# A hybrid encoder trunk: the n2 transform of its long convolution regrouped into pairs on 64x64 quarters of TensorE, in a bound order

## The chip, the cores and the metric

The kernel runs on one core of a Trainium2 chip. The metric is the device time of one execution in microseconds (us), the median of three runs. All numbers are float32; matrix products that must be accurate are done either as plain fp32 matmuls or as three fp32r products of split operands (a high part, and the low part that is left).

## What is computed

Two requests, prompt and sample, go through the same layer with the same weights:

```python
def encoder_layer(x, mem, ...):
    h = rmsnorm(x, norm_g)
    p = h @ w_in
    hy_u, hy_z, cf_a, cf_z, xa_q, xa_z = jnp.split(p, SPLITS, axis=-1)
    k2 = hyena_two_sided_filter(L, ...)
    y_hy = hyena_branch(hy_u, ..., k2, hy_skip) * jax.nn.silu(hy_z)
    y_cf = conformer_branch(cf_a, ...) * jax.nn.silu(cf_z)
    y_xa = memory_attention(xa_q, rmsnorm(mem, mem_norm_g), xa_w_kv) * jax.nn.silu(xa_z)
    mix = jnp.concatenate([y_hy, y_cf, y_xa], axis=-1)
    return x + mix @ w_out

def bidir_fftconv(u, k2, skip):
    uf = jnp.fft.rfft(uf32, n=2 * L, axis=1)
    kf = jnp.fft.rfft(k2, n=2 * L, axis=0)
    y = jnp.fft.irfft(uf * kf[None], n=2 * L, axis=1)[:, :L]
```

L is 2048, the width 1024, the Hyena branch has 512 channels; a last RMSNorm follows. The convolution is over a circle of 2L = 4096 = 64 x 64 positions. The position is 64 n1 + n2, the frequency 64 k2 + k1 (names as in the kernel), so the 4096-point transform is a 64-point transform over n1 with twiddles, and then one over n2. The two requests ride as the real and the imaginary part of one complex signal.

## The kernel before, in words

The program has three stages, one after the other, and a scheduler sets each engine's order within them.

**Stage 1** (lines 204 to 707) multiplies the normed input by `w_in`, 512 tokens at a time: three fp32r matmuls for each of eight pieces of the contraction (`proj`, lines 439 to 441). Work for VectorE (DVE), ScalarE (ACT) and GpSimd (POOL) runs beside it from two queues of closures: the 31-tap convolution, the filter (`filter_background`: a small network, `taps` at line 330, and the filter's transform over n1 at line 355, whose results ACT copies out at line 357 into the DRAM array XF), and at the end eight of the 32 steps of the signal's transform over n1 (`a_background`, line 613).

**Stage 2** (lines 717 to 918) holds three things. Attention (`attention`, line 756) runs in 16 blocks of two half-blocks; each half-block ends with the products of line 792. Between them stand the 24 other steps of the transform over n1 (`stage_a`, line 812): transpose, split, three pairs of products (`times_t1`, line 185), and two copies out of PSUM, one on DVE and one on ACT (line 827), stored to the DRAM array X1. Then comes the transform over n2 (`stage_b`, line 890), 33 steps t. A step loads the filter's column and takes its transform (`spectrum`, line 845: one fp32 matmul of 128x128 by 512 columns, and four half-tile copies on DVE and ACT into kr and ki). Then for column t, and for its mirror 64 - t, `unit` (line 831) does the forward matmul (line 833), two half-tile copies on ACT that swap real and imaginary part (835, 836), two products with kr and ki (838 on DVE, 839 on DVE or POOL), their sum on POOL (840), the inverse matmul (842) and a copy on ACT (843). ACT issues the store to the DRAM array AA (895, 899). SyncE (SP) issues the loads (869). Every third step also loads and splits a piece of `w_out` (`wo_load`, line 855).

The order of one unit is thus a chain over four engines:

```python
            nc.tensor.matmul(u, stab[:, t2, :], x, start=True, stop=True)
            nc.scalar.copy(us[0:64, :], u[64:128, :])
            nc.scalar.copy(us[64:128, :], u[0:64, :])
            nc.vector.tensor_tensor(z, u, kr, op=ALU.mult)
            e2.tensor_tensor(us, us, ki, op=ALU.mult)
            nc.gpsimd.tensor_tensor(z, z, us, op=op)
            nc.tensor.matmul(o, stab[:, t3, :], z, start=True, stop=True)
            nc.scalar.copy(out, o)
```

**Stage 3** (lines 922 to 980) has 32 steps, each for two columns n2 of both requests: the inverse transform over n1 (line 949), transposes (954), the gate, the split of the branch outputs (192 to 194), 48 fp32r matmuls with `w_out` (972 to 974), the residual, the last norm and the store. Its first loads read AA, and so wait for the last store of stage 2.

Of the kernel before, what the change touches and what calls it, by code (L numbers as in the profile page):

```python
# [35 lines left out]
def _tables():  # L36
# [11 lines left out]

    n1 = np.arange(64)
    n2 = np.arange(64)  # L50
# [26 lines left out]
    psi = 2 * np.pi * ((n2[:, None] * n2[None, :]) % 64) / 64  # L77
    cp, sp = np.cos(psi), np.sin(psi)

    def s2(cc, ss):  # L80
        return np.block([[cc, -ss], [ss, cc]])

    def s3(cc, ss):
        return np.block([[cc, ss], [-ss, cc]])

    cpr, spr = cp[:, ::-1], sp[:, ::-1]
    kz = s2(cp, sp)
    kz[64:] = 0
    th = 2 * np.pi * n2[:, None] / 128
    kh = np.zeros((128, 128))  # L90
    kh[64:, :64] = np.cos(th) * cp - np.sin(th) * sp
    kh[64:, 64:] = -np.cos(th) * sp - np.sin(th) * cp

    fr = (4 * np.arange(16)[:, None, None] + np.arange(2)[None, :, None] + 2 * np.arange(2)).reshape(-1)
    fr = np.concatenate([fr, 64 + fr])
    sf = s2(cp, sp)[fr]
    kz, kh = kz[fr], kh[fr]
    stab = np.stack([s2(cp, sp), s2(cpr, spr), s3(cp.T, sp.T), s3(cpr.T, spr.T), kz, kh, sf], axis=1)
# [3 lines left out]
        "stab": stab, "ident": np.eye(128),  # L102
# [5 lines left out]
def kernel(ctx: ExitStack, tc: tile.TileContext, a: dict):  # L108
# [23 lines left out]
    AA = dram.tile([64, 129, 512], F32, name="aa")  # L132
# [39 lines left out]
    def chans(d, g, n):  # L172

        return d[g, :, :, n * 64:(n + 2) * 64].rearrange("k c m -> c k m")
# [29 lines left out]
    with ExitStack() as c1:  # L204
# [82 lines left out]
        def filter_background():  # L287
# [42 lines left out]
            def taps(st, b, n):  # L330
# [153 lines left out]
        def hy_u(g, i):  # L484
# [7 lines left out]
            def v(tb, ps):  # L492
                gate(st["u"], tb, hy_conv(st, ps, 8 + i, tb))
                if tb == NB - 1:
                    nc.scalar.dma_start(UU[i].rearrange("c (n g t) -> c n g t", g=2, t=32)[:, :, g, :],
                                        st["u"].rearrange("p (n t) -> p n t", t=32))
# [116 lines left out]
        def a_background(n0):  # L613
# [18 lines left out]
            def mult(i):  # L632
                ss = slice(i * P, (i + 1) * P)
                px = ms(), ms()
                times_t1(px, st["h"][:, ss], st["l"][:, ss], st["uh"], st["ul"])
                for s in range(2):
# [390 lines left out]
```

## Time and profile before

| | |
|---|---|
| median of 3 runs | 2119.03 us (2109.97 to 2120.47) |
| the profiled execution | 2119.94 us, its span 2118.2 us |
| TensorE matmul (PE) busy | 1982.9 us (94%), 8866 instructions |
| DVE busy | 1262.6 us (60%), 1779 instructions |
| ACT busy | 759.2 us (36%), 1461 instructions |
| POOL busy | 890.4 us (42%), 854 instructions |
| DMA | 328.72 MB, mean 155 GB/s |

The span is the time from the first to the last instruction on the chip; the run's own time has 1.7 us more around it. A line's number is that of the kernel above. A matmul's busy time includes its way through the array, so back-to-back matmuls overlap in the records: what one costs is read from the distance of two starts. An fp32 matmul stands as two records, an fp32r one as one. PEld is the load of weights, PEq, ACTq and SPq are queues that issue. In the granted clock, 1.00 is 2.4 GHz.

### The profile page before, as it was taken

What the parts mean: (1) busy time and instruction counts of PE and PEld (TensorE: products, weight loads), DVE (VectorE), ACT (ScalarE), POOL (GpSimd) and SP (SyncE); (2) the same over time, 40 slices, a digit from 0 to 9 for tenths busy, and PEclk for the clock granted to TensorE, in tenths of its full rate; (3) what the DMA queues carried; (4) which work ended last, traced back from release to release, by engine and by line L of the source; (5) the groups of instructions that cost most, each with busy time, mean ns of one, the idle gap of its engine ahead of it and who ended that gap; (6) DMA issues with size and microseconds to landing.
All of it is one profiled execution on the core that took longest, in us unless ns stands there. A gap on an engine that the chain in (4) does not pass through costs nothing. (4 is left out here: it accounts for less than half of the span.)

```text
span 2118.2 us, 26007 instructions
## 1 busy us (share of the span) xinstructions
PE 1982.9 (94%) x8866; PEld 1499.7 (71%) x8866; DVE 1262.6 (60%) x1779; ACT 759.2 (36%) x1461; POOL 890.4 (42%) x854
## 2 busy tenths in 40 slices
PE   5999988898999999999989999999988889999998
PEld 5888877776777777777767778777533267777776
DVE  4766397979325365488889622178887624434443
ACT  5531122231424233321323421278787722222221
POOL 3433576755533211466645531166588711111110
PEclk8999999999999999999999999999999999999999
DMA  9643323332557423232422235698888785555552
GB/s 335 209 145 130 94 87 96 120 119 80 203 182 220 137 89 115 81 95 65 124 69 94 87 107 173 221 288 269 246 264 257 235 219 140 147 155 151 154 144 60
DMA packets 238558, 328.72 MB, mean 155 GB/s; under 512 B 87177, under 2 KB 117913, under 8 KB 236634
## 3 DMA queue, kind: packets, MB, share of 16 engines
q1 hardware_dynamic: 146026, 260.72, 38.7%
q10 hardware_dynamic: 87056, 54.57, 9.6%
q0 software_dynamic: 5344, 11.77, 2.1%
q8 instruction: 71, 1.16, 0.2%
q14 instruction: 61, 0.50, 0.1%
HBM read 196.37 MB, written 130.61 MB: 154 GB/s over the span
## 5 line engine op out<-in xcount | busy, mean ns | idle before, releaser
L439 PE MATMUL pj<-xh,whi 128*128 128x512 f32 (+1 forms) x1728 | 671.1, 389 | 32.1 <-ACT big L505 9.3
L440 PE MATMUL pj<-xl,whi 128*128 128x512 f32 (+1 forms) x1728 | 670.1, 388 | 8.6 <-POOL xl L410 6.6
L441 PE MATMUL pj<-xh,wlo 128*128 128x512 f32 (+1 forms) x1728 | 668.7, 387 | 0.0
L235 DVE SCALAR_TENSOR_TENSOR bg<-bg,vb,bg 128x512 f32<-128x512 f32 x480 | 415.3, 899 | 11.4 <-POOL bg L230 7.0
L439 PEld LDWEIGHTS pj<-xh,whi 128*128 128x128 f32 x1728 | 331.6, 192 | 101.5 <-ACT big L505 11.0
L440 PEld LDWEIGHTS pj<-xl,whi 128*128 128x128 f32 x1728 | 332.1, 192 | 74.2 <-POOL xl L410 7.5
L441 PEld LDWEIGHTS pj<-xh,wlo 128*128 128x128 f32 x1728 | 332.0, 192 | 66.3 <-issue 2.2
L972 PE MATMUL ms<-wo,mh 128*128 128x512 f32 x512 | 204.2, 399 | 2.2 <-ACT mh L193 2.2
L973 PE MATMUL ms<-wo,mh 128*128 128x512 f32 x512 | 201.3, 393 | 0.0
L974 PE MATMUL ms<-wo,ml 128*128 128x512 f32 x512 | 194.3, 397 | 0.2 <-POOL ml L194 0.2
L462 DVE SCALAR_TENSOR_TENSOR sm<-sm,va,sm 128x448 f32<-128x448 f32 (+1 forms) x96 | 84.2, 877 | 162.4 <-POOL sm L460 143.0
L460 POOL TENSOR_SCALAR sm<-sm,va 128x448 f32<-128x448 f32 (+1 forms) x96 | 119.9, 1249 | 120.0 <-ACT sm L453 112.7
L481 POOL TENSOR_TENSOR big<-big,sm 128x448 f32<-128x448 f32 (+1 forms) x64 | 121.7, 1904 | 112.1 <-DVE sm L464 108.7
L975 DVE TENSOR_TENSOR xr<-xr,ms 128x512 f32<-128x512 f32 x64 | 44.0, 688 | 199.2 <-PE ms L974 199.0
L200 POOL TENSOR_TENSOR ss<-ss,mhalf 128x1 f32<-128x1 f32 x32 | 17.7, 553 | 313.3 <-DVE ss L199 313.3
L453 ACT COPY sm<-pj 128x512 f32<-128x512 f32 x96 | 56.2, 586 | 222.0 <-PE pj L441 189.6
L972 PEld LDWEIGHTS ms<-wo,mh 128*128 128x128 f32 x512 | 96.9, 189 | 47.5 <-issue 24.3
L974 PEld LDWEIGHTS ms<-wo,ml 128*128 128x128 f32 x512 | 96.6, 189 | 20.9 <-DVE mf L958 0.8
L973 PEld LDWEIGHTS ms<-wo,mh 128*128 128x128 f32 x512 | 96.9, 189 | 20.0
L194 POOL TENSOR_TENSOR wlo<-sm,whi 128x512 fp32r<-128x512 f32 x50 | 79.5, 1603 | 63.2 <-ACT whi L193 37.0
L198 ACT ACTIVATE junk<-xr 128x1024 bf16<-128x1024 f32 x32 | 33.8, 1058 | 191.4 <-DVE xr L975 191.4
L840 POOL TENSOR_TENSOR z<-z,us 128x512 f32<-128x512 f32 x64 | 81.9, 1289 | 28.0 <-DVE us L839 21.9
(174 smaller groups left out, 2784.2 us busy)
## 6 DMA issues: line engine op xcount, KB each, us to landing
big<-in_xt_dram SPq DMA_DIRECT2D x32, 512.0 KB, 5.4
in<-x1d SPq DMA_DIRECT2D x128, 128.0 KB, 3.9
aa<-o ACTq DMA_DIRECT2D x64, 256.0 KB, 3.6
at<-aa SPq DMA_DIRECT2D x64, 256.0 KB, 5.1
out_dram<-xr ACTq DMA_DIRECT2D x64, 256.0 KB, 3.7
sm<-in_win_dram SPq DMA_DIRECT2D x52, 256.0 KB, 3.2
ws<-whi SPq DMA_DIRECT2D x52, 256.0 KB, 2.3
ws<-wlo SPq DMA_DIRECT2D x52, 256.0 KB, 2.2
```

The costliest lines, as they stand in the source:

```text
L194: (sub_eng or nc.gpsimd).tensor_tensor(lo, src, hi.bitcast(F32), op=ALU.subtract)
L235: nc.vector.scalar_tensor_tensor(st["a", c], st["h", c][:, k:k + TB], vb[:, 2 * k + c:2 * k + c + 1], st["a", c], op0=ALU.mult, op1=ALU.add)
L439: nc.tensor.matmul(ps[:, ts_], hi, xh[:, k, ts_], start=k == 0, stop=False)
L440: nc.tensor.matmul(ps[:, ts_], hi, xl[:, k, ts_], start=False, stop=False)
L441: nc.tensor.matmul(ps[:, ts_], lo, xh[:, k, ts_], start=False, stop=k == KC - 1)
L460: nc.gpsimd.tensor_scalar(ct[:, o:e], pt[:, o + 1:e + 1], w[1], va[:, 52 + ch:53 + ch], op0=ALU.mult, op1=ALU.add)
L462: nc.vector.scalar_tensor_tensor(ct[:, o:e], pt[:, o:e], w[0], ct[:, o:e], op0=ALU.mult, op1=ALU.add)
L481: nc.gpsimd.tensor_tensor(v, v, out, op=ALU.mult)
L840: nc.gpsimd.tensor_tensor(z, z, us, op=op)
L972: nc.tensor.matmul(po, mh[:, k, :], woh[k][:, hs], start=i == 0, stop=False)
L973: nc.tensor.matmul(po, mh[:, k, :], wol[k][:, hs], start=False, stop=False)
L974: nc.tensor.matmul(po, ml[:, k, :], woh[k][:, hs], start=False, stop=i == 7)
```

## The change

**Pairs.** The positions n2 are put in the order 0, 32, 1, 33 and so on (`_tables`), and each step of the transform over n1 ends with a butterfly on its two results, so that X1 and XF hold the sum and the difference of the columns n2 and n2 + 32. An even frequency then needs only the sums, an odd one only the differences: 32 values in place of 64, or 64 rows with real and imaginary part.

**Quarters.** The transforms over n2 are then 64x64 matmuls: `quarters` issues four of them, each on its own quarter of the array, two to a PSUM bank. There are 32 steps. A step has four quarters forward (columns t and mirror(t) together), eight for the spectrum and eight for the inverse. The spectrum comes out already laid out for the product, so there are no half-tile copies and no swap: four copies on ACT, four products on DVE, two copies on ACT of the inverse, and a sum and a difference of these on POOL.

**Order.** `in_order` chains every instruction of TensorE and of ACT within stage 2's last part to the one before it: forward of t, spectrum of t + 1, inverse of t - 1, store of t - 2. That part no longer starts inside attention's last two blocks.

**Buffers and layout.** PSUM has no bank of its own for attention's output (`tr` has four); SBUF tags are regrouped; AA has rows of 1024 elements, one store covering two columns. U is stored in two DMAs in place of one, the gate is loaded in runs of 256 bytes in place of 512 (four DMAs in place of two for two steps), and stage 3 reads the columns n and n + 32 in place of 2n and 2n + 1.

```diff
-    n2 = np.arange(64)
+    n2 = np.arange(64).reshape(2, 32).T.reshape(-1)
...
-    AA = dram.tile([64, 129, 512], F32, name="aa")
+    AA = dram.tile([64, 65, 1024], F32, name="aa")
...
+    def butterfly(a, b, px):
+
+        nc.scalar.copy(b, px[1])
+        nc.vector.tensor_tensor(a, px[0], b, op=ALU.add)
+        nc.vector.tensor_tensor(b, px[0], b, op=ALU.subtract)
...
+                butterfly(st["f", 0], st["f", 1], px)
                 for q in range(2):
-                    nc.scalar.copy(st["f", q], px[q])
                     nc.sync.dma_start(XF[n2p // 2, q * P:(q + 1) * P, :], st["f", q])
...
-        ms, tr, pa, po_ = psum(c2, ms=2, tr=3, pa=2, po=1)
+        ms, tr, pa = psum(c2, ms=2, tr=4, pa=2)
...
         def t_in():
-            return tl_("in", 8)
+            return tl_("in", 9)
...
-            for s in range(2):
-                xo = tl_("us", 4)
-                (nc.scalar.copy if s else nc.vector.tensor_copy)(xo, px[s])
-                nc.scalar.dma_start(X1[2 * n + s, 0:128, :], xo)
+            xo = t_z(), t_z()
+            butterfly(*xo, px)
+            for s in range(2):
+                nc.scalar.dma_start(X1[2 * n + s, 0:128, :], xo[s])
...
+        def quarters(banks, jobs):
+
+            n = len(jobs[0][3])
+            for j in range(n):
+                for b, c, r, ops in jobs:
+                    w, x = ops[j]
+                    nc.tensor.matmul(banks[b][c, :], w[r, :], x[r, :], start=j == 0, stop=j == n - 1)
...
+        def forward(st, t):
+            xa, xb = fetch(t, (0, 1)), fetch(mirror(t), (1, 0))
+            st["u"] = u = ms(), ms()
+            w0, w1 = stab[:, 0, :], stab[:, 1, :]
+            quarters(u, [(0, lo_, lo_, [(w0, xa)]), (0, hi_, lo_, [(w1, xb)]),
+                         (1, hi_, hi_, [(w0, xa)]), (1, lo_, hi_, [(w1, xb)])])
+
+        def multiply(st):
+            for j in range(2):
+                for b in range(2):
+                    st["z", j, b] = t_z()
+                    nc.vector.tensor_tensor(st["z", j, b], st["u"][b], st["k", j, b], op=ALU.mult)
+
+        def inverse(st, t):
+            o = pa(), pa()
+            quarters(o, [(h, c, r, [(stab[:, 4 + 2 * v + j, :], st["z", j, b]) for j in range(2)])
+                         for h, c, r, v, b in ((0, lo_, lo_, 0, 0), (0, hi_, lo_, 1, 1),
+                                               (1, lo_, hi_, 0, 1), (1, hi_, hi_, 1, 0))])
+            eo, st["y"] = tl_("o", 4, 1024), tl_("o", 4, 1024)
+            for h in range(2):
+                nc.scalar.copy(eo[:, h * TB:(h + 1) * TB], o[h])
+            for h, op in enumerate((ALU.add, ALU.subtract)):
+                nc.gpsimd.tensor_tensor(st["y"][:, h * TB:(h + 1) * TB], eo[:, 0:TB], eo[:, TB:], op=op)
+
+        def store(st, t):
+            for k, r in ((t, lo_), (mirror(t), hi_)):
+                nc.scalar.dma_start(AA[k, 0:64, :], st["y"][r, :])
+
+        def stage_b():
+
+            sts = [{} for _ in range(33)]
+            spectrum(sts[0], 0)
+            forward(sts[0], 0)
+            for t in range(33):
+                with in_order():
+                    if t < 32:
+                        if t:
+                            forward(sts[t], t)
+                        multiply(sts[t])
+                    if t < 31:
+                        spectrum(sts[t + 1], t + 1)
+                    if t:
+                        inverse(sts[t - 1], t - 1)
+                    if t > 1:
+                        store(sts[t - 2], t - 2)
+                    if t >= 9 and t % 3 == 0 and t < 32:
+                        wo_load(t // 3 - 3)
+            store(sts[31], 31)
...
-                for g in range(2):
-                    nc.sync.dma_start(g8[:, :, g, :], chans(GG, g, n))
+                for g in range(2):
+                    for q in range(2):
+                        nc.sync.dma_start(g8[:, :, g, q, :], chans(GG, g, q, n))
...
-                  ml[:, 4:8, :].rearrange("p a (g t s) -> p (a g) t s", g=2, s=2), ynv[:, :, :, 2 * n:2 * n + 2])
+                  ml[:, 4:8, :].rearrange("p a (g t s) -> p (a g) t s", g=2, s=2), ynv[:, :, :, :, n])
```

In TensorE's order before, in the middle of the transform over n2, units of several steps are mixed (`tr` holds a forward result, `pa` an inverse one, `ms` a spectrum; the numbers count tiles):

```order
L833 MATMUL tr_12249<-in_12246,stab 128x512
L833 MATMUL tr_12277<-in_12274,stab 128x512
L842 MATMUL pa_12196<-z_12192,stab 128x512
L847 MATMUL ms_12355<-in_12352,stab 128x512
L833 MATMUL tr_12294<-in_12291,stab 128x512
L842 MATMUL pa_12213<-z_12209,stab 128x512
L833 MATMUL tr_12322<-in_12319,stab 128x512
L847 MATMUL ms_12400<-in_12397,stab 128x512
```

Two forward matmuls of one step stand apart by a unit of another. The same place of the changed kernel (now `ms` holds the forward results, `tr` the spectrum, `pa` the inverse):

```order
L887 MATMUL ms_12541<-in_12535,stab 64x512
L887 MATMUL ms_12541<-in_12538,stab 64x512
L887 MATMUL ms_12542<-in_12535,stab 64x512
L887 MATMUL ms_12542<-in_12538,stab 64x512
L887 MATMUL tr_12558<-in_12555,stab 64x512 x2
L887 MATMUL tr_12559<-in_12555,stab 64x512 x2
L887 MATMUL tr_12568<-in_12555,stab 64x512 x2
L887 MATMUL tr_12569<-in_12555,stab 64x512 x2
L887 MATMUL pa_12578<-z_12486,stab 64x512
L887 MATMUL pa_12578<-z_12488,stab 64x512
L887 MATMUL pa_12579<-z_12488,stab 64x512
L887 MATMUL pa_12579<-z_12486,stab 64x512
```

Four more quarters for `pa` follow, and then the next step's forward. The inverse reads the products of the step before, which were made while the forward and the spectrum of this group ran.

In ACT's order of the changed kernel, at the same place, one step of the transform over n2 is this (`k` is the spectrum, `o` the inverse's copy and the stored result):

```order
L908 COPY k_12564<-tr_12558 128x512
L908 COPY k_12566<-tr_12559 128x512
L908 COPY k_12574<-tr_12568 128x512
L908 COPY k_12576<-tr_12569 128x512
L941 COPY o_12588<-pa_12578 128x512
L941 COPY o_12588<-pa_12579 128x512
L947 DMA aa<-o_12528 64x1024 x2
```

The store is that of the step before; its sums on POOL stand between.

In DVE's order, in the stretch where attention and the transform over n1 share the engine, the changed kernel has two instructions for a butterfly (L214, L215) where one copy stood (L827):

```order
L823 TENSOR_TENSOR ynp<-tr_11219,z_11217 128x512
L803 TENSOR_REDUCE mx_11555<-ms_11550 128x2
L214 TENSOR_TENSOR z_11322<-pa_11314,z_11323 128x512
L809 RECIPROCAL se_11534<-se_11534 128x2
L215 TENSOR_TENSOR z_11323<-pa_11314,z_11323 128x512
L816 COPY ynp<-tr_11435 128x4x128
```

Both wait for ACT's copy of the other bank, and hold back the reductions of attention that stand behind them.

## Rows read from the trace of the kernel before

**Rows 1.** Stretches: length; PE, PEld, DVE, ACT, POOL busy (count); clock; DMA share; GB/s

```profile
900.00:1236.00 336.00, 313.57 (x1348) 240.81 (x1346) 273.30 (x336) 109.42 (x155) 192.01 (x192) 0.99 0.32 93
...
1374.00:1490.00 116.00, 114.04 (x834) 82.74 (x834) 91.80 (x187) 91.00 (x304) 70.81 (x88) 0.97 0.88 275
...
1503.00:1527.00 24.00, 22.91 (x104) 11.42 (x101) 20.86 (x37) 16.37 (x41) 10.73 (x11) 1.00 0.91 283
1527.00:1694.00 167.00, 144.03 (x296) 53.25 (x294) 125.75 (x176) 127.09 (x223) 137.46 (x107) 0.96 0.80 253
...
1712.00:2118.00 406.00, 396.49 (x1756) 300.44 (x1756) 159.95 (x221) 88.58 (x157) 58.07 (x63) 0.99 0.54 143
```

**Rows 2.** The chain of waits, its piece after the last store of stage 2

```profile
1694.88 5.56 DMA aa<-o
...
1709.91 1.98 PE tr L949 x4
```

**Rows 3.** Groups by line, 1527 to 1694 us: busy us, mean ns, then idle before

```profile
L840 POOL TENSOR_TENSOR z<-z,us 128x512 f32<-128x512 f32 x61 | 78.1, 1290 | 21.8 <-DVE us L839 15.7 <-DVE z L838 1.6 <-PE ms L847 1.5
L842 PE MATMUL pa<-z,stab 128*128 128x512 f32 x122 | 67.0, 638 | 7.6 <-POOL z L840 6.2 <-ACT o L843 1.0
...
L838 DVE TENSOR_TENSOR z<-tr,k 128x512 f32<-128x512 f32 x60 | 41.1, 689 | 23.1 <-ACT us L836 17.1 <-POOL z L840 2.7 <-issue 1.3
...
L843 ACT COPY o<-pa 128x512 f32<-128x512 f32 x60 | 34.9, 586 | 14.5 <-PE pa L842 13.1 <-ACT o L843 0.4
...
L193 ACT CAST wo<-in 128x512 fp32r<-128x512 f32 x16 | 9.6, 618 | 1.7 <-DMA in<-in_w_out_dram 1.6
```

**Rows 4.** Waits, 1527 to 1694 us: total us, times, longest

```profile
PEld pa L842 <- POOL z L840: 27.9, 30, 3.9
...
DVE z L838 <- ACT us L836: 17.1, 17, 3.3
```

**Rows 5.** Timeline of PE, fp32 matmuls of full size back to back: start, length

```profile
1518.04 1.02 PE L842 MATMUL pa<-z,stab 128*128 128x512 f32 x2
1518.90 1.02 PE L847 MATMUL ms<-in,stab 128*128 128x512 f32 x2
```

**Rows 6.** Timeline of PE, two row halves in the filter's transform (771 us)

```profile
771.61 1.08 PE L355 MATMUL ms<-f,f 64*64 64x512 f32 x4
772.61 0.50 PE L336 MATMUL ms<-big 128*128 128x512 f32 x1
```

**Rows 7.** Timeline of PE, two column halves at the end of attention's half-blocks

```profile
1502.32 1.08 PE L792 MATMUL po<-ynp,wo 128*64 128x256 f32 x8
...
1505.69 1.08 PE L792 MATMUL po<-ynp,wo 128*64 128x256 f32 x8
...
1525.45 1.08 PE L792 MATMUL po<-ynp,wo 128*64 128x256 f32 x8
```

**Rows 8.** Timeline of ACT's queue, one store's issue

```profile
1601.60 0.33 ACTq L899 DMA_DIRECT2D aa<-o  x1
```

**Rows 9.** DMA issues, 1530 to 1690 us: count, KB each, median us to landing

```profile
aa<-o ACTq DMA_DIRECT2D x58, 256.0 KB, 3.5
in<-x1d SPq DMA_DIRECT2D x104, 128.0 KB, 3.7
...
in<-in_w_out_dram SPq DMA_DIRECT2D x16, 256.0 KB, 4.5
```

**Rows 10.** Busy time by stretch, two of stage 2 with dense transfers

```profile
1372.00:1400.00 28.00, 25.09 (x165) 19.15 (x166) 19.32 (x41) 21.09 (x68) 15.82 (x20) 0.88 1.01 315
...
1420.00:1440.00 20.00, 20.00 (x153) 14.22 (x154) 17.07 (x35) 15.70 (x54) 12.56 (x16) 1.00 0.92 289
```

**Rows 11.** Waits of SP's queue, 1530 to 1690 us

```profile
SPq L869 <- DMA aa<-o: 30.0, 24, 3.1
```

**Rows 12.** Groups by line on DVE, 1374 to 1490 us

```profile
L827 DVE COPY us<-pa 128x512 f32<-128x512 f32 x23 | 15.9, 690 | 0.8 <-PE pa L190 0.8
```

**Rows 13.** Groups by line on PE, 900 to 1250 us: the filter's transform

```profile
L355 PE MATMUL ms<-f,f 64*64 64x512 f32 x80 | 17.3, 625 | 6.4 <-DVE f L341 6.4
```

More of the change, by code (lines that the diff above doesn't have):

```diff
@@ L94, in _tables, with forward @@
[L94 to L98, printed above, removed]
+    jj, ab, pair = np.arange(32), np.arange(32)[:, None], np.arange(2)
+    def forward(k2, conj=1.0):
+        th = 2 * np.pi * ((ab * k2[None, :]) % 64) / 64
+        w = np.zeros((32, 2, 2, 32))
+        w[:, 0, 0], w[:, 1, 0] = np.cos(th), np.sin(th)
+        w[:, 0, 1], w[:, 1, 1] = -conj * np.sin(th), conj * np.cos(th)
+        return w.reshape(64, 64)
@@ new lines, in inverse, with both @@
+    def inverse(k2, conj, turned):
+        th = 2 * np.pi * ((k2[:, None] * ab.T) % 64) / 64
+        w = np.zeros((2, 32, 2, 32))
+        re = np.stack([np.cos(th), np.sin(th)], axis=1)
+        im = conj * np.stack([-np.sin(th), np.cos(th)], axis=1)
+        w[0], w[1] = (im, -re) if turned else (re, im)
+        return w.reshape(64, 64)
+    def both(a, b):
+        return np.concatenate([a, b], axis=0)
+    ev, od, evr, odr = 2 * jj, 2 * jj + 1, 62 - 2 * jj, 63 - 2 * jj
+    fk = both(forward(ev), forward(od))
@@ new lines, with in_order @@
+        lo_, hi_ = slice(0, 64), slice(64, 128)
+        @contextmanager
+        def in_order(engines=(nc.tensor, nc.scalar)):
+            code, n = nc.cur_bb.bb.instructions, {}
+            first = len(code)
+            yield
+            code = list(nc.cur_bb.bb.instructions)
+            for e in engines:
+                last = next((x for x in reversed(code[:first]) if x.engine == e.engine), None)
+                for x in code[first:]:
+                    if x.engine == e.engine:
+                        if last is not None:
+                            tc.add_manual_dep(x, last.name, mybir.DependencyInfo(
+                                mybir.DependencyClass.NoSync, mybir.DependencyReason.DATA), reason="in_order")
+                        last = x
@@ new lines, in quarters, with spectrum @@
+        def quarters(banks, jobs):
[4 more added lines that the diff above has]
+                    nc.tensor.matmul(banks[b][c, :], w[r, :], x[r, :], start=j == 0, stop=j == n - 1)
+        def spectrum(st, t):
+            xf = t_in()
+            src = XF[:, 0:256, :].rearrange("m (h e k) c -> m h e k c", h=2, e=4)
+            for h, r in enumerate((lo_, hi_)):
+                nc.sync.dma_start(xf[r, :], src[:, h, :, t % 32, :])
+            if t == 0:
+                sk = t_in().rearrange("p (j c) -> p j c", j=4)
+                nc.sync.dma_start(sk, a["sk"])
+            for j in range(2):
+                pk = tr(), tr()
+                if t == 0:
+                    for b in range(2):
+                        nc.tensor.matmul(pk[b], sk[:, 2 * j + b, :], xf, start=True, stop=True)
+                else:
+                    w = stab[:, 2 + j, :]
+                    quarters(pk, [(0, lo_, lo_, [(w, xf)]), (0, hi_, lo_, [(w, xf)]),
+                                  (1, lo_, hi_, [(w, xf)]), (1, hi_, hi_, [(w, xf)])])
+                for b in range(2):
+                    st["k", j, b] = t_k()
+                    nc.scalar.copy(st["k", j, b], pk[b])
```

139 lines of the change are left out of this document (51 added, 88 removed).

## The prediction

> **What bounds the kernel now.** I read the table of stretches first [rows 1]. In stage 3 (1712 to 2118 us) PE is busy 396.5 of 406 us: nothing but fewer matmuls shortens it. In attention with the transform over n1 (1374 to 1490) PE is busy 114 of 116, and DVE 91.8. In the transform over n2 (1503 to 1694) no engine is full: DVE 126 of 167, ACT 127, POOL 137, the DMA engines 0.80. PE's 144 of 167 there deceives. Two fp32 matmuls in a row start 0.86 us apart, though each record set is 1.02 long [rows 5], and the stretch holds 148 of them (122, 118 and 56 records, of which [rows 3] shows the first): 127 us of work in 167. The list of waits says what ends the rest [rows 4]: the weight load of the inverse waits 27.9 us for POOL's sum, POOL's sum for DVE, DVE's product 17.1 us for ACT's swapped copy. The stage is bound by the chain of one unit over four engines, in the order that the scheduler chose. The chain that ended last shows that its end counts in full: the last store is issued at 1694.9 us, and stage 3's first waited-for matmul follows at 1709.9 [rows 2].
>
> **The change, part by part.** *TensorE's work in a step.* A step had five full matmuls (spectrum, two forward, two inverse), 4.3 us at 0.86. It now has 20 quarters, five groups of four. The trace shows quarters in pairs only. Two row halves with different data (four records) take 1.0 us from their start to the next matmul's [rows 6], which in turn would be 1.7; in attention four matmuls of 256 columns on two column halves last 1.08 us in all [rows 7], where 256 columns at half of 0.86 four times would be 1.72. So rows work beside rows and columns beside columns. That four do is not shown; I take 0.86 a group, 4.3 us a step, against 8.6 if only two ever run together, and keep the second as a rival. The Trainium skill, TensorEngine Tiling (Array Packing), Tiling Modes, counts 64x64 as four independent tiles. By that rule a step is 4.3 us and that rival falls away; no row here shows four.
>
> *The other engines in a step.* ACT: six copies at 0.586, two issues of a store at 0.33, and half a cast of `w_out` at 0.618 [rows 3, 8]: 4.5 us. Before, its 127.1 us [rows 1] over some 30 steps were 4.2 without the issues, where it is now 3.8: the copies that the new layout saves are few. DVE: four products at 0.689, 2.8 us. POOL: two sums at 1.29 and half a split, 3.2 us. None of these needs another within the same step, since the inverse reads products of the step before: the chain of [rows 4] is off the path. The tightest loop left, forward 0.86, four products 2.76, next forward (they share two PSUM banks), is 3.6 plus hand-overs, below 4.3.
>
> *Transfers in a step.* Six loads of 128 KB and two stores of 256 KB, as before, and half a load of `w_out` [rows 9]: 1.44 MB. At 315 GB/s that is 4.6 us, at 289 GB/s 5.0: these are the densest stretches of stage 2 [rows 10]. At 253, the stage's present rate [rows 1], 5.7. The Trainium skill, DMA: Bandwidth & Descriptors, Specifications, gives a core about 358 GB/s of HBM. By that figure a step's transfers would take an estimated 4.0 us and never bind; the stretches shown stay below it.
>
> So a step costs at least 4.5 us (ACT) and at most 5.7. I take **4.7**: a little over ACT's sum and between the two dense rates, because no dependency within a step is left that is longer. Before, 148 matmuls in 167 us were 5.6 a step.
>
> *What the change loses.* The transform over n2 no longer begins inside attention. Attention's half-blocks go at 3.4 us; three are left after the one at 1505.7, though in the trace the last comes at 1525.5, held up by that work [rows 7]. Alone, attention would end at 1505.7 + 3 x 3.4 + 1.1 = 1517.
>
> *Butterflies beside attention.* 24 steps over n1 get one more DVE instruction of 0.69 [rows 12], 16.6 us on an engine that is busy 91.8 of 116 [rows 1]: 108.4, or 93 percent. It fits below PE, so the least is 0 (a gain is excluded, PE has 2 us of slack in all). In its densest stretch DVE reaches 17.07 of 20 [rows 10], and at that share it would need 127.5 us, 11.5 more. I take +4, nearer to the fit.
>
> *Butterflies in the filter.* 16 of them in stage 1, two DVE instructions of 0.69 more and one ACT copy less. PE waits there for the engine that feeds it, and lost 22 us from 900 to 1236 while DVE was 81 percent busy [rows 1]. Ten of the 16 fall there (80 records of eight each), 13.8 us of DVE. Bounds: 0 if covered by the convolution's slack, 13.8 if all on the path. The row that is nearest is PE's own wait for DVE before these matmuls, 6.4 us [rows 13]; half as much again is +3.
>
> *Start and end.* After attention: two pairs of full matmuls (1.9 us to the first result), two copies, then four products, so that the next forward starts after some 6.1 us. Behind the last forward: 0.86, products 2.76, half an inverse 0.86, copies 1.17, sums 2.58, with hand-overs 9.5 us to the store's issue. Together 15.6, and 30 steps between.
>
> *Stage 3.* The same PE work. Four gate loads in place of two, and a read of the branch outputs at a larger stride by ACT and POOL, stand where DMA is 0.54 busy and POOL 58 of 406: at nothing; even at twice its time POOL would be busy 116 of 406. Without that cover the first steps could lose 2 us. The eight more issues for U, 0.33 each on ACT in stage 1, hide under PE's projections.
>
> **Sum.** 1517 + 4 + 3 + 15.6 + 30 x 4.7 = 1680.6 for the last store's issue, against 1694.9: 14.3 us less, and stage 3 follows as it did. The profiled execution's own 2119.9 becomes 2105.6; it lies 0.9 above the median of the runs shown, so against the median I say **2105**.
>
> **The rivals.**
>
> *The gain is given back* (2121). Transfers run at 289 GB/s, 5.0 us a step, and DVE beside attention at its densest share: 1517 + 11.5 + 3 + 15.6 + 150 = 1697, 2 us later than now. For it: DMA share 0.91 to 0.92 where the rate was 283 to 289, and YN's loads fall into the first steps. Against it: 315 was reached.
>
> *Loads queue behind stores: slower* (2135). SP's loads waited 30 us, 24 times, for the landing of an earlier store to AA [rows 11]. SP issues in order, so one such wait holds every load behind it. If step for step loads and stores wait for each other's landing, 3.5 to 4.5 us each [rows 9], the rate stays at its present 253 GB/s, 5.7 us a step: 30 us more than forecast, 16 more than now. ACT would suffer twice, since copies queue behind a store that waits, and then TensorE, bound in order. It decides from 5.5 us a step. Against it: with a lag of two steps the store comes long after its sums, and nine load buffers hold more than two steps.
>
> *Only two quarters at a time: slower* (2222). 8.6 us a step, 117 more than forecast. Against it: both kinds of pair are shown.
>
> *It all fits* (2092). 4.5 us a step and no charge for butterflies: 1517 + 15.6 + 135 = 1667.6, 27.3 less. For it: nothing in the sums forbids it. Against it: PE, ACT and DMA would all be above 95 percent at once.
>
> **How the numbers follow.** A measurement of this kernel tells about 0.5% (10.6 us) from no change: faster is below 2108.4, slower above 2129.6. Forecast, 4.5 to 5.0 us a step, 2099 to 2114: 0.52, of which 0.36 lies below 2108.4. It fits: 0.09. Given back: 0.19. Queueing: 0.14. Two at a time: 0.06. So faster 0.45, same 0.35, slower 0.20. The range runs from 2090 (the fit and 2 us) to 2136 (queueing at the present rate); outside are two at a time, the worse part of queueing and a little of the fit.
>
> **What would show it.** In the new profile, the distance from one step's forward quarters to the next, 4.7 us; four quarter records starting together, and groups 0.86 apart; ACT over 90 percent busy between attention's end near 1524 us and the last store near 1681; PE's waits there on POOL gone, on ACT or DMA in their place; DVE over 90 percent busy beside attention; stage 3 again 406 us. The prediction is wrong if groups stand 1.7 apart, if SP or ACT wait for `aa` in every step, or if attention ends later than 1532.

## The result, and the profile after

The changed kernel takes 2144.03 us (median of 4 runs, 2142.70 to 2149.34), the kernel before 2114.50 beside it (4 runs, 2109.22 to 2120.47): 1.0144 times as long, 95% interval 1.0105 to 1.0183. Slower by 30 us, and 8 us above the range of the prediction. The profiled execution took 2142.89 us, its span is 2141.0.

The table of stretches, in the columns of [rows 1]: attention with the transform over n1, the first steps of the transform over n2, its later steps, stage 3.

```profile
1388.00:1504.00 116.00, 114.47 (x758) 81.53 (x758) 96.14 (x192) 86.14 (x280) 66.26 (x81) 0.97 0.76 247
1550.00:1586.00 36.00, 35.40 (x300) 16.61 (x292) 18.29 (x30) 20.39 (x41) 17.54 (x14) 1.00 0.83 249
1586.00:1705.00 119.00, 114.53 (x876) 49.61 (x874) 55.60 (x88) 75.53 (x151) 70.57 (x57) 1.00 0.86 274
1733.00:2139.00 406.00, 398.28 (x1760) 300.63 (x1760) 130.68 (x222) 104.05 (x157) 82.79 (x63) 0.99 0.58 144
```

DVE beside attention is at 96 of 116 us, not over 90 percent; ACT in the later steps is at 76 of 119, not over 90 percent either. There no engine is near its limit but the matmul records of PE, which overlap; transfers run at 274 GB/s. The chain of waits around the end of stage 2, as [rows 2]:

```profile
1716.75 0.45 ACTq L947
...
1721.01 0.38 SPq L1019
1721.39 0.05 issue
1721.44 0.50 SPq L1019
...
1733.09 1.98 PE tr L1031 x4
```

Between the two profiles the time went as follows. The last projection starts at 1384.7 us (before 1371.4): 13.3 more in stage 1. From there to the last store's issue it is 332.1 us (before 323.5): 8.6 more. From the store to stage 3's first waited-for matmul 16.3 (before 15.0): SP has two more issues for the gate, L1019. Stage 3 takes 407.9 (before 408.3). The sum is 22.8, the difference of the spans. The medians differ by 30, since the profiled execution of the kernel before, 2119.94 us, is among its slowest.

Quarters do run four at a time. The timeline of PE from the forward matmuls of step 2 to those of step 3, eight records for four quarters:

```profile
1550.92 1.04 PE L887 MATMUL ms<-in,stab 64*64 64x512 f32 x8
1551.78 1.90 PE L887 MATMUL tr<-in,stab 64*64 64x512 f32 x16
1553.49 1.90 PE L887 MATMUL pa<-z,stab 64*64 64x512 f32 x16
1555.21 1.68 PE L887 MATMUL ms<-in,stab 64*64 64x512 f32 x8
```

From one forward to the next is 4.29 us, five groups of 0.86. The list of waits, 1527 to 1714 us, against [rows 4]:

```profile
DVE z L932 <- ACT k L908: 76.6, 33, 3.8
POOL o L943 <- DMA aa<-o: 60.8, 21, 6.1
PEld tr L887 <- ACT k L908: 25.2, 50, 1.9
ACT k L908 <- PE pa L887: 18.0, 8, 3.9
...
ACT k L908 <- POOL o L943: 11.0, 3, 3.9
```

The weight loads no longer wait for POOL's sum. POOL waits for the landing of stores instead (21 times, so not in every step), DVE for ACT, and ACT, in its bound order, for PE and for POOL. SP, which waited 30.0 us for `aa` [rows 11], now waits for buffers that PE frees (12.7 us, the largest row, L915).

### The profile page after: what moved, and what is told of

Same layout as the page of the kernel before. It is cut to its first block, busy times and chain, and to the rows that moved or that the text cites. A ratio compares the mean times of both kernels' runs of the same rounds, so it can differ in the third digit from the quotient of the medians.

```text
span 2141.0 us, 27838 instructions
## 1 busy us (share of the span) xinstructions
PE 2010.9 (94%) x9816; PEld 1525.5 (71%) x9816; DVE 1209.2 (56%) x1775; ACT 745.2 (35%) x1417; POOL 867.4 (41%) x823
## 5 line engine op out<-in xcount | busy, mean ns | idle before, releaser
L464 PE MATMUL pj<-xh,whi 128*128 128x512 f32 (+1 forms) x1728 | 676.2, 392 | 44.5 <-ACT big L531 19.6
L464 PEld LDWEIGHTS pj<-xh,whi 128*128 128x128 f32 x1728 | 333.1, 193 | 115.4 <-ACT big L531 22.1
L465 PEld LDWEIGHTS pj<-xl,whi 128*128 128x128 f32 x1728 | 333.3, 193 | 75.9 <-POOL xl L435 7.2
L506 POOL TENSOR_TENSOR big<-big,sm 128x448 f32<-128x448 f32 (+1 forms) x64 | 117.3, 1833 | 104.9 <-DVE sm L489 97.8
L932 DVE TENSOR_TENSOR z<-ms,k 128x512 f32<-128x512 f32 x128 | 81.1, 685 | 86.9 <-ACT k L908 76.6
L943 POOL TENSOR_TENSOR o<-o 128x512 f32<-128x512 f32 x64 | 80.0, 1273 | 78.1 <-DMA aa<-o 60.8
```

Source lines behind the costliest of these rows:

```text
L464: nc.tensor.matmul(ps[:, ts_], hi, xh[:, k, ts_], start=k == 0, stop=False)
L465: nc.tensor.matmul(ps[:, ts_], hi, xl[:, k, ts_], start=False, stop=False)
L506: nc.gpsimd.tensor_tensor(v, v, out, op=ALU.mult)
L932: nc.vector.tensor_tensor(st["z", j, b], st["u"][b], st["k", j, b], op=ALU.mult)
L943: nc.gpsimd.tensor_tensor(st["y"][:, h * TB:(h + 1) * TB], eo[:, 0:TB], eo[:, TB:], op=op)
```

## The experiments

Each is the changed kernel with one edit, unless told otherwise. The table has, from each run's one profiled execution: stage 1 from the 433rd of its 5184 products to the last (the first 105 us differ by up to 8 us between executions of like code, and are left out); attention, from the last projection to the start of the last of attention's matmuls; and the mean distance of two forwards of the transform over n2 in steps 2 to 9 and 10 to 31. Then follow the median time of several executions and its ratio to the kernel before, measured in the same session.

| run | stage 1 | attention | steps 2-9 | 10-31 | median us | ratio (95%) |
|---|---|---|---|---|---|---|
| before | 1267.9 | 154.3 | | | 2114.5 | |
| before_again | 1268.0 | 154.7 | | | 2120.2, one run | |
| changed | 1282.0 | 157.5 | 4.72 | 5.46 | 2144.0 | 1.0144 (1.0105-1.0183) |
| u_on_sp | 1278.6 | 158.2 | 4.62 | 5.45 | 2141.9 | 1.0117 (1.0093-1.0142) |
| filter_copies | 1280.0 | 158.1 | 4.83 | 5.66 | 2143.6 | 1.0134 (1.0104-1.0164) |
| u_one_store | 1276.8 | 159.9 | 4.74 | 5.47 | 2140.0 | 1.0109 (1.0086-1.0131) |
| old_stage1 | 1267.0 | 158.0 | 4.61 | 5.51 | 2132.0 | 1.0062 (1.0044-1.0080) |
| pairs_together | 1282.1 | 146.7 | 5.31 | 5.47 | 2133.0 | 1.0084 (1.0058-1.0110) |
| both_causes | 1268.1 | 147.2 | 5.22 | 5.54 | 2123.3 | 1.0020 (1.0009-1.0030) |
| one_store | 1280.9 | 157.8 | 7.47 | 12.55 | 2365.2 | 1.1177 (1.1153-1.1202) |
| four_results | 1284.4 | 157.7 | 4.29 | 5.54 | 2147.6 | 1.0131 (1.0109-1.0154) |
| free_order | 1280.7 | 157.5 | 5.97 | 6.52 | 2181.4 | 1.0306 (1.0282-1.0330) |
| w_out_last | 1284.8 | 157.5 | 4.44 | 5.76 | 2161.1, one run | |
| w_out_on_dve | 1284.6 | 159.9 | 5.47 | 6.72 | 2172.7 | 1.0265 (1.0241-1.0290) |
| three_together | 1285.7 | 147.4 | 5.09 | 6.65 | 2165.5 | 1.0228 (1.0204-1.0252) |
| half_spectrum | 1285.4 | 160.3 | 4.47 | 5.02 | 2138.4, one run | |
| no_mirror_load | 1283.2 | 158.6 | 4.29 | 5.15 | 2135.0, one run | |
| best_three | 1281.5 | 148.1 | 4.30 | 5.63 | 2137.5 | 1.0097 (1.0083-1.0111) |
| best_two | 1280.3 | 147.3 | 4.89 | 5.54 | 2135.1 | 1.0092 (1.0078-1.0106) |

### Stage 1: the stores of U, and an order that moved

before_again is the kernel before, unedited.

> The kernel before, once more, for a second profile of it. If its first stage varies from execution to execution, the last projection starts up to 10 us away from the 1371.8 us of the first profile; if the changed kernel's 13 us there are its own, it starts again within 3 us of 1371.8.

Its stage 1 takes 1268.0 us from the 433rd product, against 1267.9 in the first profile: the changed kernel's 14 us there are its own.

u_on_sp:

```diff
-                        nc.scalar.dma_start(UU[i].rearrange("c (n q g t) -> c n q g t", q=2, g=2, t=32)[:, :, q, g, :],
+                        nc.sync.dma_start(UU[i].rearrange("c (n q g t) -> c n q g t", q=2, g=2, t=32)[:, :, q, g, :],
```

> The changed kernel with the two stores of U (line 521) issued by SP in place of ACT. Theory 1 (the second of the two issues, 3.2 to 3.5 us on ACT's queue, holds back the copies that TensorE waits for): the last projection starts some 8 us earlier than 1384.7 us, TensorE's waits on ACT's gate activation fall from 41.7 us to some 20, the time is some 8 us below the changed kernel's. Theory 2 (the butterflies of the filter cost stage 1 its 13 us): stage 1 stays within 2 us.

filter_copies:

```diff
-                butterfly(st["f", 0], st["f", 1], px)
                 for q in range(2):
+                    nc.scalar.copy(st["f", q], px[q])
```

> The changed kernel with two ACT copies in place of each of the 16 butterflies of the filter, which leaves out the sums and differences of the filter's columns. Theory 1 (stores of U): stage 1 is at most 3 us shorter. Theory 2 (butterflies of the filter): stage 1 is some 10 us shorter, its end near 1374 us.

Neither alone settled it: 3.4 and 2.0 us of 14. What u_on_sp was to test can be read from ACT's timeline. The changed kernel at the fourth store of U:

```profile
421.23 3.98 ACTq L521 DMA_DIRECT2D uu<-big  x2
425.26 1.99 ACT L531 ACTIVATE big<-pj 128x512 f32<-128x512 f32 x2 [15.22 <-issue]
```

The kernel before at the same place:

```profile
418.40 0.52 ACTq L495 DMA_DIRECT2D uu<-big  x1
418.97 1.98 ACT L505 ACTIVATE big<-pj 128x512 f32<-128x512 f32 x2 [11.70 <-POOL big L481]
```

The first of the two issues takes 0.52 us, the second, right behind it, 3.42. The gate's activation, and with it a PSUM bank, comes that much later: PE waits longer there, first the changed kernel, then the one before:

```profile
PE pj L464 <- ACT big L531: 10.5, 1, 10.5
```

```profile
PE pj L439 <- ACT big L505: 6.6, 1, 6.6
```

The mean granted clock from 410 to 430 us is 0.74 against 0.83, between the two levels of 1.00 and 0.50 (2.4 and 1.2 GHz): more of these 20 us passed at the lower one, with PE busy 9.4 of them against 13.4. On SP the second issue takes 3.5 us as well, but no longer holds ACT: the waits for this activation over stage 1 fall from 41.7 us (PE 19.6, its weight loads 22.1) to 11.6. Stage 1 still kept 10.7 of its 14 us, so this wait is a part of the loss and not all of it.

old_stage1 takes all of stage 1's edits back (the one of filter_copies, and the two that follow), u_one_store the first of these two, that of U, alone:

```diff
-                    for q in range(2):
-                        nc.scalar.dma_start(UU[i].rearrange("c (n q g t) -> c n q g t", q=2, g=2, t=32)[:, :, q, g, :], ...
+                    nc.scalar.dma_start(UU[i].rearrange("c (n g t) -> c n g t", g=2, t=32)[:, :, g, :], ...
...
-                butterfly(*xo, px)
+                    (nc.scalar.copy if s else nc.vector.tensor_copy)(xo[s], px[s])
```

> The changed kernel with stage 1 as it was before in its instructions: one store of U, two ACT copies in place of each butterfly of the filter, an ACT and a DVE copy in place of each of the eight butterflies at its end. This leaves U's columns in the old order, and leaves out sums and differences of the filter and of a quarter of X1. TensorE's order in stage 1 is then that of the kernel before. Theory 1 (the order that the scheduler makes, moved by these edits, costs stage 1 its 13 us): the last projection starts at 1372 to 1375 us, the time is some 10 us below the changed kernel's. Theory 2 (it is chance from execution to execution): it starts near 1384 as before.

> The changed kernel with U stored by one DMA again, which leaves U's columns in the old order (of the 14 to 15 us that stage 1 takes back with all its old instructions, this is the part of U alone; the butterflies stay). Theory 1 (the second issue behind the first, 3.2 to 3.5 us on ACT, and the order that follows from it): from the 432nd product of the projections to the last the changed kernel takes 1282.0 us, this one 1274 to 1277. Theory 2 (the butterflies are nearly all of it): 1280 to 1282.

With the old instructions stage 1 takes 1267.0 us, the whole 15 back, and the median falls by 12. By stretches of the projections: from the 433rd to the 2593rd product (before 566.9 us) the changed kernel takes 574.1, u_one_store 567.1: 7 us are U's stores. u_on_sp takes 570.4 there, so 3.7 of the 7 go with the hold on ACT; where the other 3.3 come from is open. From there to the 4897th, where the filter's transform stands (before 624.7), the changed kernel takes 629.5, u_one_store 631.4, filter_copies 628.9, old_stage1 624.4: 5 to 7 us that go only when both edits go. In this stretch filter_copies has TensorE's order of before, row for row, and is 4.5 us longer than old_stage1 all the same, so U's two stores cost time there without a change of TensorE's order. With the butterflies the order differs, and how much of u_one_store's 7 us is order and how much DVE's time was not tried. From the 4897th to the last (before 76.2), every kernel with the eight butterflies at stage 1's end takes 78.4, old_stage1 75.9.

### Attention: two row halves that no longer run together

The end of attention was forecast at 1524 us and came at 1543.0; 10.3 of the difference come from stage 1. PE's timeline of the changed kernel, rows of the transform over n1 alone:

```profile
1469.01 0.50 PE L209 MATMUL pa<-k,th 64*128 64x512 f32 x1
1469.35 0.40 PE L209 MATMUL pa<-k,tl 64*128 64x512 f32 x1
1469.59 0.39 PE L209 MATMUL pa<-k,th 64*128 64x512 f32 x1
...
1471.41 0.50 PE L209 MATMUL pa<-k,th 64*128 64x512 f32 x1
...
1475.48 0.51 PE L209 MATMUL pa<-k,th 64*128 64x512 f32 x2
```

A step is three products on each half of the rows. In the third of these groups both halves start together (x2). In the first two, one step's halves run alone, with other matmuls between: 0.9 us of TensorE more. Of 144 matmuls of the 24 steps, 76 start alone, and 6 in the kernel before; that is 12 steps, 10.8 us. TensorE's order shows it: three matmuls for one bank, then twelve others, then three for the other bank (the first of these is the last row):

```order
L209 MATMUL pa_10328<-k_10324,th_10315 128x512
L209 MATMUL pa_10328<-k_10324,tl_10316 128x512
L209 MATMUL pa_10328<-k_10325,th_10315 128x512
L202 MATMUL tr_10432<-ident,o_10311 128x128 x4
L799 MATMUL ms_10550<-wo_9986,wo_9999 128x256 x4
L202 MATMUL tr_10464<-ident,o_10456 128x128 x4
L209 MATMUL pa_10329<-k_10324,th_10315 128x512
```

The butterfly frees one bank at ACT's copy and the other at its second DVE instruction, where two copies had freed both nearly at once.

pairs_together: the first of the six products of a step is held until that DVE instruction of the step before.

```diff
...
             times_t1(px, th, tl, uh, ul)
+            if freed:
+                x = next(x for x in list(nc.cur_bb.bb.instructions)[first:] if x.engine == nc.tensor.engine)
+                tc.add_manual_dep(x, freed[-1], mybir.DependencyInfo(
+                    mybir.DependencyClass.Sync, mybir.DependencyReason.DATA), reason="freed")
             xo = t_z(), t_z()
             butterfly(*xo, px)
+            freed.append(next(x for x in reversed(list(nc.cur_bb.bb.instructions)) if x.engine == nc.vector.engine).name)
```

> The changed kernel, with the first product of each step over n1 in stage 2 held until the second PSUM bank is free, so that the two row halves stand together in TensorE's order. Theory 1 (in 12 of 24 steps the two halves run one after the other, 0.9 us each): attention and the transform over n1 take some 149 us from the last projection in place of 159, the time is some 9 us lower. Theory 2 (DVE, with one more instruction a step, sets the pace): within 2 us of the changed kernel, or slower.

Attention takes 146.7 us, 10.8 less, and the median falls by 11. The agreement of these two numbers is partly chance: in the profile steps 2 to 9 go from 4.72 to 5.31 us, and from the last projection to the last store's issue only 5.1 us are gained (327.0 against 332.1); most of the rest lies in the first 105 us, which differ between executions. Its PE timeline has all six together:

```profile
1468.36 0.50 PE L209 MATMUL pa<-k,th 64*128 64x512 f32 x2
1468.70 0.39 PE L209 MATMUL pa<-k,tl 64*128 64x512 f32 x2
1468.93 0.39 PE L209 MATMUL pa<-k,th 64*128 64x512 f32 x2
```

No matmul of these starts alone now. The second DVE instruction remained, so DVE did not set the pace. both_causes joins the edits of old_stage1 and pairs_together; with the sums and differences that it leaves out it shows where the time goes and is no version to use.

> The changed kernel with stage 1's old instructions (as in old_stage1, with what that leaves out) and row halves held together in the transform over n1 (as in pairs_together). If the two causes add and the rest of stage 2 goes by its bytes: stage 1 ends at 1368 to 1371 us, attention takes 147 us more, the last store is issued near 1697, and the time is 2117 to 2122 us, that of the kernel before within its range: the regrouped transform itself then gains and loses nothing. If the step of the transform over n2 lengthens by what attention gives up: 2125 us or more.

2123.3 us, 1.0020 times the kernel before (1.0009 to 1.0030), between the two figures expected: of the 30 us the two account for 26 by the ratios, each taken beside the kernel before, and for 21 by the medians alone. Stage 2 is 5.7 us shorter than in old_stage1 (328.0 against 333.7 from last projection to last store), not 10.8: steps 2 to 9 go from 4.61 to 5.22 and take half back.

### The transform over n2: stores, order, bytes

one_store:

```diff
-            for k, r in ((t, lo_), (mirror(t), hi_)):
-                nc.scalar.dma_start(AA[k, 0:64, :], st["y"][r, :])
+            m = mirror(t)
+            nc.scalar.dma_start(AA[t:m + 1:m - t, 0:64, :], st["y"])
```

> The changed kernel with one DMA of 512 KB in place of two of 256 KB for each step's store to AA, so that a step has seven DMAs on eight completion lanes and no store follows a store on its lane. Theory 1 (ACT waits at the store for the landing of the store before, and copies, products and quarters queue behind it): a step goes from 5.27 us to some 4.8, the time is 10 to 15 us lower. Theory 2 (the transfers' rate sets the step): a step stays at 5.2 to 5.3, the time within 3 us. Theory 3 (POOL's sum waits for the landing because only two result tiles exist): a step stays or gets longer, since one landing of 512 KB comes later than the first of two.

A step got longer, which only the third theory allowed, and the lane was not tested. The one DMA moves 50 GB/s while it is alone, so that POOL waits up to 10.7 us for its landing. The busy share of the 16 DMA engines, in tenths, and the rate, 1700 to 1726 us in 40 slices:

```profile
DMA  7311111111111357757511111211111167761689
GB/s 249 136 50 57 50 50 50 50 50 57 50 57 50 120 189 236 255 211 224 189 57 50 50 50 50 76 54 54 50 57 57 63 221 217 236 221 63 214 290 353
```

From 1703.5 to 1708.5 us the mean share is 0.13, two of sixteen. The Trainium skill, DMA: Bandwidth & Descriptors, in its section on why a DMA increments its semaphore by 16, spreads a DMA over the largest number of engines, up to 16, that divides the size of the slowest dimension on both sides; on the side of AA that size is 2 here. The share and the 50 GB/s agree, and the expectation had not reckoned with it. The waits, 1600 to 1900 us, show who hangs on a landing:

```profile
POOL o L943 <- DMA aa<-o: 218.4, 24, 10.7
DVE z L932 <- ACT k L908: 186.4, 21, 11.7
ACT k L908 <- DMA in<-x1d: 131.8, 13, 11.2
```

four_results is to take that wait away, with a part of the branch outputs' space as two more result tiles:

```diff
-                        nc.sync.dma_start(ynp[:, c, gg, :], YN[gg][c])
+                        if (c, gg) != (1, 1):
+                            nc.sync.dma_start(ynp[:, c, gg, :], YN[gg][c])
...
-            eo, st["y"] = tl_("o", 4, 1024), tl_("o", 4, 1024)
+            eo = tl_("o", 4, 1024)
+            st["y"] = ynp[:, 1, 1, t // 2 % 2 * 1024:][:, 0:1024] if t % 2 and t < 28 else tl_("o", 4, 1024)
...
+                    if t == 29:
+                        nc.sync.dma_start(ynp[:, 1, 1, :], YN[1][1])
```

> The changed kernel with four tiles for the results of a step in place of two: every second result of the steps up to 27 is made in a part of the space that holds the branch outputs later, whose load follows at step 29. Theory 1 (POOL's sum waits for the landing of the store two steps before, and the store that waits for POOL holds back ACT): POOL's 60.8 us of waits for aa fall below 15, a step goes from 5.46 us in steps 9 to 31 to some 5.0, the time is 8 to 12 us lower. Theory 2 (transfers' rate, 274 GB/s): a step stays within 0.1 us. Theory 3 (the completion lane: ACT's store itself waits for the landing of the store before): ACT's waits for aa stay, a step falls by 0.2 at most.

POOL's waits for `aa` fall from 60.8 us to one of 1.7, and steps 2 to 9 take 4.29 us, the sum of the quarters. Steps 10 to 31 stay (5.54): where the wait ended, another took its place. ACT's own waits for `aa` stay, some 11 us before and after, as the third theory said; what they cost was not tried apart. Two things limit what steps 2 to 9 show. The edit also moves a load of 1 MB of the branch outputs from the start of the transform to step 29, some 4 us at the 268 GB/s of this stretch, about the 3.4 us gained. And no_mirror_load, below, has two result tiles still, yet fewer bytes: its steps 2 to 9 take 4.29 us too, with no wait of POOL for `aa` in them. So the wait is not shown to be a cause apart from the bytes. Steps of 4.29 us ask for 305 GB/s, more than the 268 that were moved; nine load tiles of 256 KB, filled ahead, can lend the difference of 1.3 MB for eight steps, and not for thirty (an estimate).

free_order (`in_order(())`):

> The changed kernel without the binding of TensorE's and ACT's order in the transform over n2. Theory 1 (bound in order, TensorE and ACT queue behind a store that waits): the scheduler's own order is as fast or faster, a step 5.0 to 5.3 us. Theory 2 (the bound order is what keeps the steps apart): a step over 5.6 us, the time more than 10 us higher.

5.97 and 6.52 us a step, the median 37 us higher: the bound order is worth more than the waits that it hands on.

w_out_on_dve, and three_together with it:

```diff
-                split(woh[k][:, hs], wol[k][:, hs], raw)
+                nc.vector.tensor_copy(woh[k][:, hs], raw)
+                nc.vector.tensor_tensor(wol[k][:, hs], raw, woh[k][:, hs].bitcast(F32), op=ALU.subtract)
```

> The changed kernel with the splits of w_out in the transform over n2 on DVE (cast and difference) in place of ACT and POOL. Theory 1 (their time on ACT and POOL, in a bound order): steps 9 to 31 fall from 5.46 us to some 5.0, the time is some 10 us lower. Theory 2 (the transfers, 272 GB/s with w_out in it): they stay within 0.1 us.

> The changed kernel with row halves held together in the transform over n1, four result tiles, and the splits of w_out on DVE. If the three are independent, attention takes 147 us, the first eight steps 4.3 us each and the others as in the run with w_out on DVE alone or less: 2118 to 2125 us. If a transfer's rate bounds the steps, they stay at 5.4 and the time is 2130 to 2135.

Both miss. DVE has time, but its order is not bound: the cast stands ahead of products and waits there for its load. The waits, 1600 to 1740 us, of w_out_on_dve:

```profile
DVE wo L974 <- DMA in<-in_w_out_dram: 37.4, 7, 6.2
```

w_out_last (the eight `wo_load` behind the loop), then two that take bytes alone away, half_spectrum (the filter's column loaded at even t only and used twice) and no_mirror_load:

```diff
-            xa, xb = fetch(t, (0, 1)), fetch(mirror(t), (1, 0))
+            xa = xb = fetch(t, (0, 1))
```

> The changed kernel with the loads and splits of w_out moved behind the transform over n2, so that its 32 steps hold nothing else (the time itself then has them at the end in the open). Theory 1 (the share of w_out, its two casts on ACT, two differences on POOL, half a megabyte and two load buffers in every third step, is what lifts a step from 4.7 in the first eight to 5.46): steps 9 to 31 take 4.3 to 4.8 us. Theory 2 (the loop of stores and sums): they stay at 5.2 to 5.5.

> The changed kernel, with the filter's column loaded in every second step only and used twice, which leaves out half of the filter: 1.354 MB a step on average in steps 9 to 31 in place of 1.485, all engines' work alike. Theory 1 (the transfers' rate, 1.485 MB in 5.46 us or 272 GB/s, is what a step waits for): these steps take 1.354 MB at 272 GB/s, 4.98 us, and the rate stays between 262 and 280. Theory 2 (the bound order with its waits for stores, sums and casts): 5.3 us or more, and the rate falls to 255 or less.

> The changed kernel with the mirrored column not loaded, the column itself used in its place, which leaves out half of the transform's input: 1.223 MB a step in steps 9 to 31. Theory 1 (rate): 1.223 MB at 272 GB/s, 4.50 us, which is also ACT's sum of a step, so 4.5 to 4.8 us. Theory 2 (order): 5.2 us or more.

The stretches, one row from each (w_out_last, half_spectrum, no_mirror_load):

```profile
1586.00:1690.00 104.00, 101.82 (x824) 47.93 (x820) 50.62 (x81) 64.66 (x122) 50.37 (x41) 1.00 0.85 262
```

```profile
1588.00:1700.00 112.00, 110.21 (x900) 44.08 (x896) 56.76 (x91) 74.89 (x149) 72.48 (x59) 0.98 0.87 271
```

```profile
1588.00:1700.00 112.00, 102.56 (x870) 41.85 (x864) 53.73 (x87) 72.50 (x145) 70.82 (x58) 0.98 0.75 222
```

w_out_last fits neither figure: steps 10 to 29 take 5.09 us (the last two wait for the loads that were moved), which is 1.31 MB at 262 GB/s, 5.0. half_spectrum takes 5.02 where 4.98 was expected from bytes, at an unchanged rate. So as it stands a step goes with its bytes, at 262 to 274 GB/s, in one profile each. What holds the rate there is not parted: SP, which alone issues these loads, is issuing for 94.7 of the 110 us from 1590 to 1700 in the changed kernel, 87.7 in half_spectrum and 60.8 in no_mirror_load, so its work falls with the bytes, and no run moved loads to another queue. no_mirror_load takes 5.15, not 4.50, and its rate falls to 222: below some 5 us another limit shows. Up to step 13 its steps take 4.29; from step 17 on they take 4.3 to 5.7 us, but one in three, at the loads of `w_out`, 6.6 to 8.6. SP then issues nothing until POOL's first difference of an earlier piece, which ends at 1658.8 us, sets free the tile for its next load. SP's queue, and below it POOL:

```profile
1651.15 2.57 SPq L973 DMA_DIRECT2D in<-in_w_out_dram  x2
1658.85 1.18 SPq L915 DMA_DIRECT2D in<-x1d  x2
```

```profile
1657.56 2.50 POOL L219 TENSOR_TENSOR wo<-in,wo 128x512 fp32r<-128x512 f32 x2
```

### A better version

best_three has row halves together, four results and U's two stores on two queues; best_two leaves the results out.

> A version of the changed kernel: row halves held together in the transform over n1, four result tiles, and the two stores of U on two queues, ACT's and SP's. If the gains add: 11 us from attention, 3 to 5 from stage 1, nothing from the result tiles alone: 2127 to 2132 us, still 10 us over the kernel before, whose stage 2 moved its 84.5 MB at 262 GB/s already.

> The same without the four result tiles: 2127 to 2132 us, within 3 us of the version with them if the steps go by the transfers' rate; 4 us or more above it if POOL's waits for the landing of stores count once attention ends sooner.

They took 2137.5 and 2135.1, above both ranges and no better than pairs_together; the four results are worth nothing in the whole time. Issued on two queues at once, U's two stores take 0.55 us each in place of 0.52 and 3.5, yet stage 1 is only 0.5 and 1.7 us shorter. No version with the regrouped transform beat the kernel before.

## Why the prediction was wrong

**What bounds the kernel now**: right that stage 2's end counts in full, and that the chain over four engines [rows 4] held the transform. It missed that stage 2 as a whole stood near what its transfers allow: some 84.5 MB from last projection to last store, 262 GB/s before and 253 after. At the 274 of the later steps these bytes take 308 us, against 323.5 before.

**Quarters**: 0.86 us a group, as taken, 4.29 for five; "two at a time" is out. The Trainium skill, TensorEngine Tiling (Array Packing), Tiling Modes, counts 64x64 tiles as four independent ones, and the trace agrees: four matmul records start within 0.02 us of each other, at 1550.92 and again at 1551.35.

**The step, 4.7**: failed at 5.26 (steps 2 to 31). The engines' sums held, as steps of 4.29 in four_results and no_mirror_load show; the rate of the transfers did not. Of 289 to 315 GB/s from short dense stretches, 274 was reached over 119 us. The row to take was in the same table, a rate held for a hundred microseconds: 275 GB/s over 116 us of attention [rows 1]. At it the bytes of a step, 1.31 MB in steps 2 to 9 and 1.49 in steps 10 to 31, where all of `w_out` falls, take 4.8 and 5.4 us; 4.72 and 5.46 were measured. 30 steps, 17 us. That the bytes set the step is the reading that fits; SP's issues and the load tiles fall with the bytes, and were not tried apart. The Trainium skill, DMA: Bandwidth & Descriptors, Specifications, names about 358 GB/s a core; the densest stretch read here had 315 [rows 10].

**Loads behind stores**: a part was right (POOL and ACT wait for `aa`), its price was not: that wait was worth at most 0.4 us a step in steps 2 to 9, and nothing later.

**Butterflies beside attention, +4**: wrong in kind. From the last projection to attention's end 145.2 us were forecast without a charge (1517 - 1371.8), and pairs_together takes 147.0, so the butterflies' time on DVE cost some 2 us at most; but the butterfly moved TensorE's order, 10.8 us. The order of the changed kernel had shown it ahead of any run; I read DVE's order there, not TensorE's.

**Butterflies in the filter, +3**: stage 1 lost 14. Of these 7 are the stores of U, which I hid at 0.33 us an issue under PE's projections. The price was that of another DMA [rows 8]; eight of sixteen took 3.2 to 3.5, and what hides on an engine that is 36 percent busy is late when TensorE waits for that engine. 5 us more lie beside the filter's transform, from the stores and the butterflies together. The eight butterflies at stage 1's end stood in no term; they took 2.2.

**Start, end, stage 3**: 15.8 us for 15.6, by luck: the next forward starts 3.6 us after attention's end and not 6.1, since the first matmuls of step 0 still stand ahead of attention's last half-block (from 1536.2 us); and from the last forward to the store's issue it is 12.2 us, not 9.5. Stage 3 takes 407.9 where it was 408.3, and the gate's loads 1.3 us ahead of it. The sum of the misses, 10.3 in stage 1, 8.7 in attention, 16.9 in the steps and 0.2 in start and end, is 36.1: 1680.6 became 1716.7.

## What to carry to other kernels

Look at what a bank's release does to the order on TensorE: two operations that free two banks at different times can part two half-array matmuls that ran together. Before a chain of engines is shortened, divide the stage's bytes by a rate that some long stretch has held; at that rate regrouping gains no more than the difference to the present time, here some 15 us of 323. And price a DMA's issue with what stands right before it on its queue: the same store of U took 0.52 us to issue by itself and 3.5 behind another like it.

## What the runs showed of the hardware

Two DMAs of 4096 runs of 128 bytes, issued one behind the other on ACT's queue, took 0.52 and 3.2 to 3.5 us to issue; on SP's queue the same (0.52 and 3.5, u_on_sp); at once on the two queues 0.55 each (best_two); one DMA of 8192 such runs took 0.52. A store of 512 KB whose outermost destination dimension is 2 moved 50 GB/s while alone, with 0.13 of the 16 DMA engines busy, where two of 256 KB, in the changed kernel, landed in 4.6 us each. Three matmuls on one half of the rows, followed in TensorE's order by three on the other half, started in pairs (1475.48, x2): the fourth in the order started 10 ns after the first and ahead of the second, so adjacency of the two groups was enough and alternation was not needed.
